# Instance norm on one core: storing finished units two at a time, in transfers of 8 MB

## The chip, the cores and the metric

The kernel runs on 1 core of one Trainium2 chip. The metric is device time in microseconds (us), the median of repeated runs. Lower is better. A transfer between device memory (HBM) and on-chip memory (SBUF) is carried by the core's 16 DMA engines, which all instructions that issue transfers share.

## The reference

Each of the 4 x 8 x 16 = 512 channels of `x` is a plane of 256 x 256 float32 values. Each plane is normalised by its own mean and variance and multiplied by one number of `gamma`:

```python
def reference(x, gamma):                  # x: (4, 8, 16, 256, 256), gamma: (8, 16)
    mu = x.mean(axis=(3, 4), keepdims=True)
    var = ((x - mu) ** 2).mean(axis=(3, 4), keepdims=True)
    x_norm = (x - mu) / np.sqrt(var + 1e-5)
    return (x_norm * gamma[None, :, :, None, None]).astype(np.float32)
```

So 134.2 MB are read and 134.2 MB are written, and every plane has to be on the chip as a whole before its first output value is known.

## The kernel before, in words

**Tiling.** The input is cut into U = 32 units of 16 planes. A plane is spread over S = 8 partitions, so a unit fills 128 partitions with F = 8192 values each: 32 KB a partition, 4 MB in all. A unit is one contiguous 4 MB piece of HBM, in the input and in the output alike.

**Buffers.** There are AHEAD = 6 slots of one unit each (`xt`). Unit u lives in slot u % 6 from its load until its store has landed, and the result is written over the input.

**Loads (L48).** The first six loads are issued at the start, those of units 1 and 3 from ScalarE's queue and the other four from SyncE's (SP). Inside the loop, SP issues the load of unit u + 6 after the store of unit u; since it fills the same slot, it waits until that store has landed. SP has no other work, and the order of its loads is the order of the units.

**Work on a unit.** VectorE sums the unit (L102) while ScalarE squares it and sums the squares (L103, its elementwise output goes to a scratch tile `junk`). A small matmul (L111) adds up the 8 partitions of each plane and hands the result to all 8. Then come four steps of one number a partition: the negated variance (L112, VectorE), its square root (L116, ScalarE), the reciprocal (L120) and the product with gamma (L122, both VectorE). Last, VectorE writes the scaled unit in place (L125).

**Stores (L129).** ScalarE's queue issues the store of unit u when L125 has finished. The next unit's squares (L103) stand behind it on ScalarE.

The instructions of each engine run in the order in which the loop writes them. Waits are on semaphores, which a transfer raises when its data have landed. Each transfer is cut by its partitions over the 16 DMA engines: 8 rows of 32 KB for each engine, and one small packet that raises the semaphore. There are two rings of such work at each DMA engine, one for SP's issues (queue q1 in the profile) and one for ScalarE's (q10).

Of the kernel before, what the change touches and what calls it, by code (L numbers as in the profile page):

```python
# [1 line left out]

# [4 lines left out]

F32 = mybir.dt.float32
U8 = mybir.dt.uint8
ALU = mybir.AluOpType  # L10
ACTF = mybir.ActivationFunctionType
AX = mybir.AxisListType


@with_exitstack
def kernel(
    ctx: ExitStack,
    tc: tile.TileContext,
    x: bass.AP,
    gamma: bass.AP,  # L20
    out: bass.AP,
):
    nc = tc.nc
    B, G, C, H, W = x.shape
    P = nc.NUM_PARTITIONS
    HW = H * W
    n_ch = B * G * C
    S = 8
    K = P // S
    F = HW // S  # L30
    U = n_ch // K
    NG = (G * C) // K
    AHEAD = 6
    assert HW % S == 0 and (G * C) % K == 0

    xv = x.rearrange("b g c h w -> (b g c h w)").rearrange("(u p f) -> u p f", p=P, f=F)
    ov = out.rearrange("b g c h w -> (b g c h w)").rearrange("(u p f) -> u p f", p=P, f=F)
    gv = gamma.rearrange("g c -> (g c)")

    data = ctx.enter_context(tc.tile_pool(name="data", bufs=1))  # L40
    singles = ctx.enter_context(tc.tile_pool(name="singles", bufs=1))
    psum = ctx.enter_context(tc.tile_pool(name="psum", bufs=4, space=bass.MemoryType.PSUM))
    ctx.enter_context(tc.manual_schedule())

    slots = [data.tile([P, F], F32, name=f"xt{i}") for i in range(AHEAD)]

    def load(u, queue):
        queue.dma_start(out=slots[u % AHEAD][:], in_=xv[u])  # L48


    g_row = singles.tile([1, G * C], F32, name="g_row")
    nc.gpsimd.dma_start(out=g_row[:], in_=gv[None, :])  # L52
    for u in range(AHEAD):
        load(u, nc.scalar if u in (1, 3) else nc.sync)


    eps_t = singles.tile([P, 1], F32, name="eps_t")
    nc.gpsimd.memset(eps_t[:], 1e-5)  # L58
    one = singles.tile([1, 1], F32, name="one")
    nc.gpsimd.memset(one[:], 1.0)  # L60
    navg = singles.tile([P, K, S], F32, name="navg")
    nc.gpsimd.memset(navg[:], -1.0 / HW)  # L62
    nc.gpsimd.affine_select(  # L63
        out=navg[:], in_=navg[:], pattern=[[-S, K], [0, S]], compare_op=ALU.is_ge,
        fill=0.0, base=0, channel_multiplier=1,
    )
    nc.gpsimd.affine_select(  # L67
        out=navg[:], in_=navg[:], pattern=[[S, K], [0, S]], compare_op=ALU.is_ge,
        fill=0.0, base=S - 1, channel_multiplier=-1,
    )  # L70
    navg_w = navg[:].rearrange("p k s -> p (k s)")
    root_eps = singles.tile([P, 1], F32, name="root_eps")
    nc.scalar.activation(out=root_eps[:], in_=eps_t[:], func=ACTF.Sqrt)  # L73
    g_rep = singles.tile([1, NG, K, S], F32, name="g_rep")
    g_ps = psum.tile([P, NG], F32, name="g_ps", bufs=1)
    g_col = singles.tile([P, NG], F32, name="g_col")

    nc.vector.tensor_copy(  # L78
        out=g_rep[:],
        in_=g_row[:].rearrange("o (n k) -> o n k", n=NG).unsqueeze(3).to_broadcast([1, NG, K, S]),  # L80
    )
    for n in range(NG):
        nc.tensor.matmul(  # L83
            out=g_ps[:, n : n + 1],
            lhsT=g_rep[:, n].rearrange("o k s -> o (k s)"),
            rhs=one[:],
            start=True, stop=True,
        )
    nc.vector.tensor_copy(out=g_col[:], in_=g_ps[:])  # L89

    junk = singles.tile([P, F], U8, name="junk")

    st = singles.tile([P, U, 2], F32, name="st")
    nvar = singles.tile([P, U], F32, name="nvar")
    std = singles.tile([P, U], F32, name="std")
    rstd = singles.tile([P, U], F32, name="rstd")
    scale = singles.tile([P, U], F32, name="scale")

    squares = []
    for u in range(U):  # L100
        t = slots[u % AHEAD]
        nc.vector.reduce_sum(out=st[:, u, 0:1], in_=t[:], axis=AX.X)  # L102
        square = nc.scalar.activation(  # L103
            out=junk[:], in_=t[:], func=ACTF.Square, accum_out=st[:, u, 1:2],
        )
        if u:

            tc.declare_no_dep(square.ins, squares[-1].ins, reason="junk, ordered by the root between")
        squares.append(square)
        ps = psum.tile([P, 2], F32, name="ps")  # L110
        nc.tensor.matmul(out=ps[:], lhsT=navg_w, rhs=st[:, u], start=True, stop=True)  # L111
        nc.vector.tensor_scalar(  # L112
            out=nvar[:, u : u + 1], in0=ps[:, 0:1], scalar1=ps[:, 0:1],
            scalar2=ps[:, 1:2], op0=ALU.mult, op1=ALU.add,
        )
        nc.scalar.activation(  # L116
            out=std[:, u : u + 1], in_=nvar[:, u : u + 1], func=ACTF.Sqrt,
            bias=eps_t[:], scale=-1.0,
        )
        nc.vector.reciprocal(out=rstd[:, u : u + 1], in_=std[:, u : u + 1])  # L120
        g = u % NG
        nc.vector.tensor_mul(  # L122
            out=scale[:, u : u + 1], in0=rstd[:, u : u + 1], in1=g_col[:, g : g + 1],
        )
        nc.vector.tensor_scalar(  # L125
            out=t[:], in0=t[:], scalar1=ps[:, 0:1], scalar2=scale[:, u : u + 1],
            op0=ALU.add, op1=ALU.mult,
        )
        nc.scalar.dma_start(out=ov[u], in_=t[:])  # L129
        if u + AHEAD < U:  # L130
            load(u + AHEAD, nc.sync)


# [1 line left out]
_INS = ['x', 'gamma']  # L135
_OUTS = [((4, 8, 16, 256, 256), 'float32')]


# [23 lines left out]
```

## Time and profile before

| what | value |
|---|---|
| median of 3 runs | 626.83 us (626.78 to 626.91) |
| span of the profiled execution, first to last instruction | 625.2 us |
| median less span: what lies around the instructions | 1.6 us |
| VectorE busy | 443.2 us (71%) |
| ScalarE busy | 238.8 us (38%) |
| TensorE busy | 21.4 us (3%) |
| moved by DMA | 268.46 MB, 429 GB/s over the span |
| mean of one L102, L103, L125 | 8.68, 7.03, 4.55 us |
| stores: count, size, median from issue to landing | 32, 4 MB, 62.5 us |
| loads: count, size, median from issue to landing | 32, 4 MB, 38.5 us (SP's 30) |

The profiled execution has no time of its own beside its span, so the 1.6 us around it are the difference to the median of the runs. In the profile, "busy" is the time in which an engine executes; the time from issue to landing of a transfer holds its wait behind earlier transfers of the same ring. The chain of waits is followed back from the last instruction, and each of its pieces says when it began, how long it lasted, and what it was.

### The profile page before, as it was taken

The page shows a single profiled execution, that of the slowest core. Times are in us where ns is not written, and L with a number is a line of the kernel's source. Part 1 is how long each engine was busy: PE and PEld are TensorE (multiplying, and loading weights), DVE is VectorE, ACT ScalarE, POOL GpSimd, SP SyncE. Part 2 cuts the span into 40 slices and gives each one's busy share as a digit, 9 for nine tenths or more (in the row PEclk, how much of TensorE's full clock was granted, in tenths as well). Part 3 has the DMA queues.
Part 4 walks back from the last instruction along what each step waited for, and adds up shares of the span by engine and source line. Part 5 has one row for each costly group of instructions (what it writes and reads, how often), then busy time and mean ns, then how long its engine had stood idle before and what let it go on. Part 6 is the DMA issues. An engine that isn't in the chain of part 4 may idle for free.

```text
span 625.2 us, 627 instructions
## 1 busy us (share of the span) xinstructions
PE 21.4 (3%) x80; PEld 19.6 (3%) x80; DVE 443.2 (71%) x162; ACT 238.8 (38%) x98; POOL 1.9 (0%) x10
## 2 busy tenths in 40 slices
PE   2000000000000000000000000000000000000000
PEld 2000000000000000000000000000000000000000
DVE  0588999999776687666786767867668676687730
ACT  0444444444443244432344423444224442244400
POOL 1000000000000000000000000000000000000000
DMA  8999999999999999999999999999999999999998
GB/s 369 436 403 436 436 436 436 436 426 432 434 434 436 424 434 436 436 434 436 436 421 434 434 434 432 432 434 436 436 434 436 436 419 434 434 436 432 432 434 369
DMA packets 9251, 268.46 MB, mean 429 GB/s; under 512 B 1057, under 2 KB 1057, under 8 KB 1057
## 3 DMA queue, kind: packets, MB, share of 16 engines
q10 hardware_dynamic: 4896, 142.61, 52.9%
q1 hardware_dynamic: 4320, 125.83, 46.8%
q14 instruction: 3, 0.02, 0.0%
q0 software_dynamic: 32, 0.00, 0.0%
HBM read 134.22 MB, written 134.22 MB: 429 GB/s over the span
## 4 chain that ended last, share of the span: by engine, by line
another core or an unknown queue 61%; DMA 17%; DVE 15%; SPq 1%; PE 1%; issue 0%; ACT 0%
DMA xt<-in_x_dram 10%; DVE st L102 10%; DMA out_dram<-xt 8%; DVE xt L125 5%; SPq L48 1%; PE ps L111 1%; ACT std L116 0%; DVE nvar L112 0%; DVE rstd L120 0%; DVE scale L122 0%
## 5 line engine op out<-in xcount | busy, mean ns | idle before, releaser
L102 DVE TENSOR_REDUCE st<-xt 128x1 f32<-128x8192 f32 x32 | 277.9, 8684 | 105.3 <-DMA xt<-in_x_dram 105.3
L103 ACT ACTIVATE junk<-xt 128x8192 uint8<-128x8192 f32 x32 | 224.9, 7029 | 275.4 <-DMA xt<-in_x_dram 232.2
L125 DVE TENSOR_SCALAR xt<-xt,ps,scale 128x8192 f32<-128x8192 f32 x32 | 145.6, 4550 | 1.2
L116 ACT ACTIVATE std<-nvar,eps_t 128x1 f32<-128x1 f32 x32 | 9.4, 294 | 79.7 <-DVE nvar L112 79.7
L111 PE MATMUL ps<-st,navg 128*128 128x2 f32 x64 | 17.9, 349 | 562.0 <-DVE st L102 562.0
L111 PEld LDWEIGHTS ps<-st,navg 128*128 128x128 f32 x64 | 16.1, 312 | 563.8 <-issue 563.8
L112 DVE TENSOR_SCALAR nvar<-ps 128x1 f32<-128x1 f32 x32 | 9.2, 287 | 23.9 <-PE ps L111 23.9
L120 DVE RECIPROCAL rstd<-std 128x1 f32<-128x1 f32 x32 | 5.3, 164 | 11.6 <-ACT std L116 11.6
L78 DVE COPY g_rep<-g_row 1x1024 f32<-1x1024 f32 x1 | 0.7, 683 | 10.6 <-DMA g_row<-in_gamma_dram 10.6
L103 ACT ACTIVATION_READ_ACCUMULATOR junk<-xt 128x1 f32 x32 | 6.0, 186 | 0.0
L122 DVE TENSOR_TENSOR scale<-rstd,g_col 128x1 f32<-128x1 f32 x32 | 5.1, 159 | 1.1
L83 PE MATMUL g_ps<-one,g_rep 1*128 1x1 f32 x16 | 3.5, 347 | 11.5 <-DVE g_rep L78 11.5
L83 PEld LDWEIGHTS g_ps<-one,g_rep 1*128 1x128 f32 x16 | 3.5, 326 | 11.4 <-issue 11.4
L89 DVE COPY g_col<-g_ps 128x8 f32<-128x8 f32 x1 | 0.2, 167 | 3.7 <-PE g_ps L83 3.7
L73 ACT ACT_TABLE_LOAD x1 | 1.3, 1283 | 1.7 <-PEq L146 1.7
L52 POOL DMA_DIRECT2D g_row<-in_gamma_dram x1 | 0.6, 607 | 0.8 <-POOLq L146 0.8
L63 POOL TENSOR_SCALAR_AFFINE_SELECT navg<-navg 128x128 f32<-128x128 f32 x1 | 0.4, 398 | 0.1
L67 POOL TENSOR_SCALAR_AFFINE_SELECT navg<-navg 128x128 f32<-128x128 f32 x1 | 0.4, 398 | 0.1
L62 POOL MEMSET navg<- 128x128 f32 x1 | 0.2, 230 | 0.0
L73 ACT ACTIVATE root_eps<-eps_t 128x1 f32<-128x1 f32 x1 | 0.2, 203 | 0.0
L58 POOL MEMSET eps_t<- 128x1 f32 x1 | 0.1, 118 | 0.0
L146 POOL MEMSET const-bfloat16-1.0<- 128x1 bf16 x1 | 0.1, 102 | 0.0
(4 smaller groups left out, 0.4 us busy)
## 6 DMA issues: line engine op xcount, KB each, us to landing
out_dram<-xt ACTq DMA_DIRECT2D x32, 4096.0 KB, 62.5
xt<-in_x_dram SPq DMA_DIRECT2D x30, 4096.0 KB, 38.5
xt<-in_x_dram ACTq DMA_DIRECT2D x2, 4096.0 KB, 31.8
g_row<-in_gamma_dram POOLq DMA_DIRECT2D x1, 0.5 KB, 9.3
```

Source lines behind the costliest of these rows:

```text
L48: queue.dma_start(out=slots[u % AHEAD][:], in_=xv[u])
L73: nc.scalar.activation(out=root_eps[:], in_=eps_t[:], func=ACTF.Sqrt)
L78: nc.vector.tensor_copy(out=g_rep[:], in_=g_row[:].rearrange("o (n k) -> o n k", n=NG).unsqueeze(3).to_broadcast([1, NG, K, S]),)
L83: nc.tensor.matmul(out=g_ps[:, n : n + 1], lhsT=g_rep[:, n].rearrange("o k s -> o (k s)"), rhs=one[:], start=True, stop=True,)
L102: nc.vector.reduce_sum(out=st[:, u, 0:1], in_=t[:], axis=AX.X)
L103: square = nc.scalar.activation(out=junk[:], in_=t[:], func=ACTF.Square, accum_out=st[:, u, 1:2],)
L111: nc.tensor.matmul(out=ps[:], lhsT=navg_w, rhs=st[:, u], start=True, stop=True)
L112: nc.vector.tensor_scalar(out=nvar[:, u : u + 1], in0=ps[:, 0:1], scalar1=ps[:, 0:1], scalar2=ps[:, 1:2], op0=ALU.mult, op1=ALU.add,)
L116: nc.scalar.activation(out=std[:, u : u + 1], in_=nvar[:, u : u + 1], func=ACTF.Sqrt, bias=eps_t[:], scale=-1.0,)
L120: nc.vector.reciprocal(out=rstd[:, u : u + 1], in_=std[:, u : u + 1])
L122: nc.vector.tensor_mul(out=scale[:, u : u + 1], in0=rstd[:, u : u + 1], in1=g_col[:, g : g + 1],)
L125: nc.vector.tensor_scalar(out=t[:], in0=t[:], scalar1=ps[:, 0:1], scalar2=scale[:, u : u + 1], op0=ALU.add, op1=ALU.mult,)
```

## The change

The six slots of one unit become three tiles of two units each; `slot(u)` names the half of such a pair that unit u lives in. The work on a unit is the same, on the same engines and in the same order. What differs is when transfers are issued and how large they are:

- An even unit is no longer stored when it is finished. After the odd unit of a pair is finished, one transfer stores both (8 MB). Its output side is written as partition, unit, value, so that each partition's row of 64 KB in SBUF goes to two rows of 32 KB that lie 4 MB apart in HBM.
- The two loads that refill the pair's tile are still 4 MB each. SP issues both after the store of the pair, and both wait for it to land.
- The last two units, 30 and 31, are stored one by one.

The first six loads, and the queues that issue them, stay as they were. There are 17 stores in place of 32, and 32 loads as before.

```diff
-    slots = [data.tile([P, F], F32, name=f"xt{i}") for i in range(AHEAD)]
+    pairs = [data.tile([P, 2, F], F32, name=f"xt{i}") for i in range(AHEAD // 2)]
+
+    def slot(u):
+        return pairs[u // 2 % (AHEAD // 2)][:, u % 2]
 
     def load(u, queue):
-        queue.dma_start(out=slots[u % AHEAD][:], in_=xv[u])
+        queue.dma_start(out=slot(u), in_=xv[u])
...
-        nc.scalar.dma_start(out=ov[u], in_=t[:])
-        if u + AHEAD < U:
-            load(u + AHEAD, nc.sync)
+        if u >= U - 2:
+            nc.scalar.dma_start(out=ov[u], in_=t)
+        elif u % 2:
+            nc.scalar.dma_start(
+                out=ov[u - 1 : u + 1].rearrange("u p f -> p u f"), in_=pairs[u // 2 % (AHEAD // 2)][:],
+            )
+            for v in (u - 1 + AHEAD, u + AHEAD):
+                if v < U:
+                    load(v, nc.sync)
```

In the changed kernel the load is line L51, the single store L133, the pair's store L135, and the in-place scaling L128.

More of the change, by code (lines that the diff above doesn't have):

```diff
@@ L100 @@
     for u in range(U):
-        t = slots[u % AHEAD]
-        nc.vector.reduce_sum(out=st[:, u, 0:1], in_=t[:], axis=AX.X)
+        t = slot(u)
+        nc.vector.reduce_sum(out=st[:, u, 0:1], in_=t, axis=AX.X)
         square = nc.scalar.activation(
-            out=junk[:], in_=t[:], func=ACTF.Square, accum_out=st[:, u, 1:2],
+            out=junk[:], in_=t, func=ACTF.Square, accum_out=st[:, u, 1:2],
         )
@@ L125 @@
         nc.vector.tensor_scalar(
-            out=t[:], in0=t[:], scalar1=ps[:, 0:1], scalar2=scale[:, u : u + 1],
+            out=t, in0=t, scalar1=ps[:, 0:1], scalar2=scale[:, u : u + 1],
             op0=ALU.add, op1=ALU.mult,
         )
-        nc.scalar.dma_start(out=ov[u], in_=t[:])
-        if u + AHEAD < U:
-            load(u + AHEAD, nc.sync)
+        if u >= U - 2:
[7 more added lines that the diff above has]
+                    load(v, nc.sync)
 _INS = ['x', 'gamma']
```

## The prediction

> **What bounds the kernel now.** I read the page's DMA rows first, because 268 MB in 625 us is a rate that may leave nothing over.
>
> ```profile
> span 625.2 us, 627 instructions
> ...
> DMA packets 9251, 268.46 MB, mean 429 GB/s; under 512 B 1057, under 2 KB 1057, under 8 KB 1057
> ...
> q10 hardware_dynamic: 4896, 142.61, 52.9%
> q1 hardware_dynamic: 4320, 125.83, 46.8%
> ...
> out_dram<-xt ACTq DMA_DIRECT2D x32, 4096.0 KB, 62.5
> xt<-in_x_dram SPq DMA_DIRECT2D x30, 4096.0 KB, 38.5
> ```
>
> The two rings' packets take 52.9 + 46.8 = 99.7% of the time of all 16 DMA engines. Whatever VectorE (71% busy) and ScalarE (38%) do is hidden; the kernel is a stream of 64 transfers of 4 MB, and only time in which the DMA engines have nothing to do can be won or lost. The last rows say that this cannot easily happen: a store lands 62.5 us after its issue, so there is always a queue. (The GB/s of the page's 40 slices jump between 436 and lower values because whole rounds of packets are counted; I read no stall from them.)
>
> Second, the chain of waits, for the pace in the middle and for the end:
>
> ```profile
> 159.90 0.33 SPq L48
> 160.23 18.97 another core or an unknown queue
> 179.20 0.02 SPq L48
> ...
> 179.25 0.33 SPq L48
> ```
>
> SP issues a load each time a store lands, and 179.25 - 159.90 = 19.35 us pass between two such landings. In each period one load and one store go through, so a transfer of 4 MB costs 9.68 us. 64 x 9.68 = 619.5 us of the span of 625.2. Of the other 5.7 us, 1.8 pass before the first packet (the packet records begin there, for loads issued at 0.81), and the rest are slow packets at the start and around 41 us, the last landing and the closing instructions. "An unknown queue" is the store ring.
>
> Third, the timeline at the start and at the end, for what the change moves:
>
> ```profile
> 37.82 0.35 ACTq L129 DMA_DIRECT2D out_dram<-xt  x1
> ...
> 52.76 0.35 ACTq L129 DMA_DIRECT2D out_dram<-xt  x1
> ...
> 67.69 0.34 ACTq L129 DMA_DIRECT2D out_dram<-xt  x1
> ...
> 78.04 4.55 DVE L125 TENSOR_SCALAR xt<-xt,ps,scale 128x8192 f32<-128x8192 f32 x1
> 81.96 0.33 SPq L48 DMA_DIRECT2D xt<-in_x_dram  x1
> ...
> 82.62 0.34 ACTq L129 DMA_DIRECT2D out_dram<-xt  x1
> ...
> 600.59 0.34 ACTq L129 DMA_DIRECT2D out_dram<-xt  x1
> ```
>
> The stores of units 0, 1, 2 and 3 are issued at 37.82, 52.76, 67.69 and 82.62: here VectorE sets the pace, one unit in 14.93 us. At 81.96 SP issues the load of unit 7, because the store of unit 1 has just landed. By then exactly eight transfers have gone through: loads 0 to 5 and stores 0 and 1. At the end the last store is issued at 600.59 and lands at 624.2, or 23.6 us later, where 9.7 would do alone: the ring still had a backlog of 14 us.
>
> **The change part by part.**
>
> *Fifteen stores fewer.* The bytes and the 32 KB packets stay; 15 x 16 semaphore packets go. In the stretch after 585 us only stores run, and there the packet records of one engine start 1.209 us apart inside a store and 1.215 us apart over the boundary of two stores. So a boundary costs 0.006 us, and 15 of them 0.09 us: -0.1. From below, even if all of the 0.3% in which the rings' packets do not fill the engines were boundaries, it would be 0.3% x 625.2 = 1.9 us for 64 transfers, 0.44 us for 15. I take -0.1, the row being the thing itself.
>
> The Trainium skill, DMA: Bandwidth & Descriptors, section on the anatomy of one DMA, fits a transfer as about 2.0 us fixed plus bytes over 436 GB/s; put on this sum it would make 15 transfers fewer worth 30 us. The trace disagrees for a ring that is never empty: 0.006 us.
>
> *The first pair's store waits for unit 1.* It is issued at about 52.8 in place of 37.82 and 52.76. The six loads keep the engines busy past that (48 rounds of 1.21 us and the start: to about 61 us), so nothing idles here. After it, loads and this store together are the same eight transfers as above. They pass through the engines without a gap, so they end when they did before: packets end on the 16 engines at 80.6 to 81.4 (mean 81.0), the landing is seen at 81.9.
>
> *The rings are then empty.* Before, three more transfers were waiting at this point: load 6 (issued when store 0 landed, at about 62.6), store 2 (67.69), and store 3 coming. After, load 6 waits for the whole pair, so SP issues it only at about 81.96 and load 7 some 0.33 us later; and units 2 and 3 leave together, not before unit 3 is scaled, at 78.04 + 4.55 = 82.6. The first load of the kernel was issued at 0.81 and its first packet began at 1.81, so an issue takes 1.0 us to reach the engines when they are idle. Load 6 starts at 81.96 + 1.0 = 83.0, store 2+3 at 82.62 + 1.0 = 83.6. The engines idle from 81.0 in the mean to 83.0: 2.0 us. This lies fully on the path, since DMA is work that nothing later can make up. If the single ring of loads (42 to 54 us) or the pair's store alone (61 to 81) should run slower than two rings do, which the trace shows only for stores, the landing would come later and the loss would grow to 83.6 - 81.0 = 2.6 and no further, until that delay itself passes 2.6. From below: 81.96 + 1.0 less the last engine's end at 81.4 is 1.6 us.
>
> *Restart.* The first packets of the kernel took 1.21 to 2.10 us, in the mean about 0.4 us more than the steady 1.213. After a pause of 2 us I expect less than from cold; 0 to 0.9 us, I take 0.2.
>
> *Later rounds.* The second rotation: pair 2 (units 4 and 5) is scaled at 82.6 + 2 x 14.93 = 112.5, while the store of pair 1 cannot land before 83.0 + 38.7 = 121.7. So the next store is in the ring 9 us before the previous one lands, and covers the 1.6 us in which SP sees the landing and gets a load to the engines. The third: pair 3 at 142.4 against a landing of pair 2 at about 161. In steady state a tile's cycle is three pairs, 3 x 38.7 = 116 us, and it needs 38.7 for its loads, 15.1 for the last unit, and 38.7 for its store: 92.5. The 23 us left are the time that stores wait in the ring, against a hand-over of 1.6. Cost nothing; if this cover were gone, each of the 13 hand-overs would cost about 2 us.
>
> *Issue on ScalarE.* A store's issue takes 0.34 us of its queue, with the next unit's squares behind it; 15 issues go, and one of two rows per partition may take up to twice as long. ScalarE is done 1.3 us before VectorE in each unit (7.03 + 0.19 us against 8.68), so either is hidden. SP's second load stands behind the first (0.33 us) and is hidden by the first one's 9.68 us.
>
> *The end.* Units 30 and 31 leave singly as before. With about 23 us of stores queued when the last one is issued, nothing idles: 0.
>
> *Rows 4 MB apart.* A store now jumps 4 MB in HBM between packets. At the start of the trace loads 0 and 1 ran side by side on the two rings, 4 MB apart in the input row by row, with packets of 1.213 us, the same as everywhere. I take 0. A page speaks against the change: the same DMA page, section on latency and other measured facts, lists a per-partition pitch of 4 MiB at half rate (103 against 214 GB/s); by it 30 units of stores would take 30 x 9.68 = 290 us more. I hold the row against it: here the pitch is between successive packets of 32 KB, not between partitions, and the two loads side by side show no slowing.
>
> **Sum.** Against the profiled execution: 625.2 - 0.1 + 2.0 + 0.2 = 627.3 us of span, and with the 1.6 us around it 628.9 us. The parts give 626.83 - 0.44 + 1.6 = 628.0 to 626.83 + 2.6 + 0.9 = 630.3. A measurement of this kernel can tell about 0.2%, or 1.25 us, from no change.
>
> **The rivals.**
>
> *Nothing to see (626.8 to 628.0).* If the issue reaches waiting engines much faster than at the cold start, in 0.3 us, the loss is 81.96 + 0.3 - 81.0 = 1.3 us less the boundaries; or if unit 3 were stored 2 us earlier, the rings would not run dry. For it: only one start stands behind the 1.0 us. Against: landing and SP's wake-up alone take 0.9 us after the mean engine's end. About 627.6; chance 0.15.
>
> *Faster: larger stores run better.* If each store taken away saved more than 2.1 / 15 = 0.14 us, the saving would outweigh the gap; at 0.25 us it would be 3.75, giving 626.83 - 3.75 + 2.2 = 625.3. For it: a store's end leaves the engines spread over nearly 1 us. Against: the other ring's packets fill that, and the boundary reads 0.006 us. Chance 0.05.
>
> *Slower by more: the store itself is slowed.* If packets that alternate between two places took 2% longer, 30 units x 9.68 x 2% = 5.8 us come on top: 634.7. Every 0.4% costs 1.2 us. For it: no store in this trace alternates. Against: the two loads side by side. Or a hand-over opens more than once, at 2 us each. Chance 0.10.
>
> **How the numbers follow.** The forecast, one gap of about 2 us, has 0.70 and 628.0 to 630.3. The range takes half of the first rival and the lower edge of the last: 627.3 to 630.8. Slower by over 0.2% (above 628.1): nearly all of the forecast and the last rival, 0.79; within: 0.16; faster: 0.05.
>
> **What would show it.** Right: the timeline shows SP issuing two loads at about 82.0 and 82.3 and no DMA packets between about 81.4 and 83; afterwards landings of pairs 38.7 us apart, and every later landing shifted by about 2.1 us; the two rings' shares sum to about 99.4%. Wrong: pair landings clearly over 38.8 us apart (the store is slowed), under 38.6 (boundaries cost more than I read), a gap at a second landing, or the first pair's store landing well after 82.

## The result, and the profile after

The changed kernel takes 641.09 us (median of 5 runs, 640.01 to 643.47) against 626.83 before: a ratio of 1.0233, 95% interval 1.0218 to 1.0249. The forecast of 628.9 had the sign and the first mechanism right, and missed some 12 us. The profiled execution has a span of 639.4 us, 14.2 more than before. How far the runs lie apart is news too: 3.5 us here, 0.14 before.

The gap came where it was expected. The timeline of the changed kernel at the end of the eighth transfer (start us, duration us, instruction):

```profile
77.89 4.55 DVE L128 TENSOR_SCALAR xt<-xt,ps,scale 128x8192 f32<-128x8192 f32 x1
81.87 0.80 SPq L51 DMA_DIRECT2D xt<-in_x_dram  x2
...
82.48 0.40 ACTq L135 DMA_DIRECT2D out_dram<-xt  x1
```

Both loads are issued at 81.87 and the store of units 2 and 3 at 82.48, when nothing is left in either ring. The windows around it, first of the kernel before, then of the changed one (the last two columns are the mean busy share of the 16 DMA engines and GB/s):

```profile
81.00:83.00 2.00, 0.00 (x0) 0.00 (x0) 2.00 (x2) 0.00 (x0) 0.00 (x0) 1.00 0.84 360
83.00:88.00 5.00, 0.00 (x0) 0.00 (x0) 5.00 (x1) 5.00 (x1) 0.00 (x0) 1.00 0.98 419
```

```profile
81.00:83.00 2.00, 0.00 (x0) 0.00 (x0) 2.00 (x2) 0.08 (x1) 0.00 (x0) 1.00 0.57 147
83.00:88.00 5.00, 0.00 (x0) 0.00 (x0) 5.00 (x1) 5.00 (x1) 0.00 (x0) 1.00 0.88 301
```

Two microseconds are a coarse window for packets of 1.2; the packet records say 2.01 us without a packet in the mean of the 16 engines. The window after it is the first surprise: the engines are 88% busy and still move only 301 GB/s. The restart is slow.

The larger surprise stands in a window over the middle of the run. Before, then after:

```profile
118.00:620.00 502.00, 14.53 (x52) 13.05 (x52) 354.19 (x130) 187.72 (x78) 0.00 (x0) 1.00 1.00 433
```

```profile
118.00:620.00 502.00, 14.51 (x52) 13.03 (x52) 349.96 (x130) 187.62 (x78) 0.00 (x0) 1.00 1.00 425
```

The DMA share is 1.00 in both. No engine idles, and yet 8 GB/s are gone: 8 / 433 x 502 = 9.3 us. The same bytes, in the same 8192 packets of 32 KB, keep the engines busy for longer. The DMA rows of the page answer to those of before:

```profile
span 639.4 us, 587 instructions
...
DMA packets 9010, 268.46 MB, mean 420 GB/s; under 512 B 816, under 2 KB 816, under 8 KB 816
...
q10 hardware_dynamic: 4656, 142.61, 52.1%
q1 hardware_dynamic: 4320, 125.83, 47.0%
...
xt<-in_x_dram SPq DMA_DIRECT2D x30, 4096.0 KB, 41.8
out_dram<-xt ACTq DMA_DIRECT2D x15, 8192.0 KB, 44.9
```

The 241 small packets fewer are there (9251 to 9010), so the change did what it says. The two rings still fill 52.1 + 47.0 = 99.1% of the engines' time, now of a longer span. The loads' ring has the same 4320 packets as before and takes 47.0% of 639.4 us where it took 46.8% of 625.2: 300.5 us for each engine in place of 292.6.

From the records of single packets the 14.2 us come apart as follows. A packet of 32 KB takes 1.213 us in the steady state of both kernels; "slow" is what a packet takes above that, summed and divided by 16 engines.

| part | before | after | difference |
|---|---|---|---|
| no packet on the engines around 81 us | 0 | 2.0 | 2.0 |
| slow packets up to 80 us (the start, the first store) | 1.4 | 1.6 | 0.2 |
| slow packets at the restart, 80 to 90 us | 0.0 | 1.4 | 1.3 |
| slow packets from 120 us on | 0.1 | 8.9 | 8.8 |
| engines done before the last one, at the end | 0.5 | 2.1 | 1.6 |

That makes 13.9 of the 14.2; the rest is not assigned. The slow packets from 120 us on come in bursts near the landing of a pair's store, of up to 38 packets over the 16 engines; about 7 of the 8.9 us lie in the ten microseconds before it lands, so most bursts begin before SP issues the next loads. About three in four of the slow packets are loads that are still under way. A packet in a burst takes 1.3 to 2.9 us.

### The profile page after: what moved, and what is told of

It reads as the page before. It is cut to its first block, busy times and chain, and to the rows that moved or that the text cites. A ratio compares the mean times of both kernels' runs of the same rounds, so it can differ in the third digit from the quotient of the medians.

```text
span 639.4 us, 587 instructions
## 1 busy us (share of the span) xinstructions
PE 21.4 (3%) x80; PEld 19.5 (3%) x80; DVE 443.3 (69%) x162; ACT 238.5 (37%) x98; POOL 1.9 (0%) x10
## 2 busy tenths in 40 slices
DMA packets 9010, 268.46 MB, mean 420 GB/s; under 512 B 816, under 2 KB 816, under 8 KB 816
## 3 DMA queue, kind: packets, MB, share of 16 engines
q10 hardware_dynamic: 4656, 142.61, 52.1%
q1 hardware_dynamic: 4320, 125.83, 47.0%
## 4 chain that ended last, share of the span: by engine, by line
DMA 59%; DVE 27%; another core or an unknown queue 9%; PE 1%; issue 1%; ACT 1%; SPq 0%
DMA xt<-in_x_dram 31%; DMA out_dram<-xt 27%; DVE st L105 18%; DVE xt L128 9%; PE ps L114 1%; ACT std L119 1%; DVE nvar L115 1%; DVE rstd L123 0%; DVE scale L125 0%; SPq L51 0%
## 5 line engine op out<-in xcount | busy, mean ns | idle before, releaser
L128 DVE TENSOR_SCALAR xt<-xt,ps,scale 128x8192 f32<-128x8192 f32 x32 | 145.6, 4551 | 1.2
L123 DVE RECIPROCAL rstd<-std 128x1 f32<-128x1 f32 x32 | 5.2, 164 | 11.6 <-ACT std L119 11.6
```

The costliest lines, as they stand in the source:

```text
L128: nc.vector.tensor_scalar(out=t, in0=t, scalar1=ps[:, 0:1], scalar2=scale[:, u : u + 1], op0=ALU.add, op1=ALU.mult,)
```

## The experiments

Each is a small edit of the changed kernel, unless it says otherwise. Times are medians against runs of the kernel before on the same chip. "Middle" is the GB/s of the window from 118 to 620 us, read as above (433 before, 425 after).

**The same schedule with stores of 4 MB.** In place of the pair's store:

```diff
+            for v in (u, u - 1):
+                nc.scalar.dma_start(out=ov[v], in_=slot(v))
```

The odd unit goes first, so that the even unit's refill, which SP issues first, still waits for the whole pair.

> The pair still leaves at once and its loads still wait for the whole pair, but as two stores of 4 MB (odd unit first), each contiguous in HBM, in place of one of 8 MB. Theory A (the schedule slows it: the load ring runs dry at each hand-over, and packets are slow when it starts again): as the changed kernel, 639 to 643 us, with 8 to 12 us of slow packets per engine. Theory B (the large store is slow in itself, because its packets alternate between rows 4 MB apart or because there are 16 rows per engine): 628 to 630 us, the gap at 81 us alone being left.

Measured: 631.16 us, ratio 1.0063 (1.0048 to 1.0079), middle 433. The rows and the waits are the same; one transfer has become two, which also puts the rows in another order (see below). 10 of the 14 us are gone. Between 80 and 90 us it still has 1.8 us without packets and 1.5 us of slow ones; after 90 us the slow ones come to 0.1 us. SP's issues at the hand-overs show it; two of the changed kernel, then the same two of this run:

```profile
158.84 0.82 SPq L51 DMA_DIRECT2D xt<-in_x_dram  x2
...
551.98 0.86 SPq L51 DMA_DIRECT2D xt<-in_x_dram  x2
```

```profile
160.08 0.86 SPq L51 DMA_DIRECT2D xt<-in_x_dram  x2
...
547.32 0.80 SPq L51 DMA_DIRECT2D xt<-in_x_dram  x2
```

Ten hand-overs lie between: 38.72 us for each with two stores, exactly four transfers of 9.68, and 39.31 with one. The schedule theory falls: the waits are the same here, and no bursts come of them. Its premise fails too, already in the changed kernel. When SP issues the two loads at 158.84, the second load of the pair before has not landed yet; VectorE can begin on that unit only at 170.14:

```profile
158.84 0.82 SPq L51 DMA_DIRECT2D xt<-in_x_dram  x2
...
170.14 8.69 DVE L105 TENSOR_REDUCE st<-xt 128x1 f32<-128x8192 f32 x1 [4.81 <-DMA xt<-in_x_dram]
```

So the load ring is not dry at this hand-over. By the landing records it had run dry at the one before (last load landed at 122.6, next issued at 123.91), and at none after it.

With the even unit's store first, its refill leaves earlier:

> As the run of two contiguous stores a pair, but the even unit's store goes first and its load waits for it alone, so that one load is issued about 10 to 19 us before the other and the load ring need not run dry. Theory A (load ring runs dry): most of the slow packets go, 628 to 631 us. Theory B (large store): 628 to 630 us as well; it differs from theory A only through the run in which both loads wait.

Measured: 629.32 us, but from 627.32 to 633.72; ratio 1.0043 (1.0022 to 1.0064), middle 433. No bursts, as both theories said. The records of this execution (span 631.2) lose 5.9 us at the end, where the engines finish up to 7 us apart. In this execution the loss is a spread of the engines and not of the packets; the other runs left no records.

**Is it the jump of 4 MB?** Three runs. The stores were written elsewhere in the output, once with the two rows of a partition 33 KB apart, once with the second unit 36 KB further on:

```diff
-                out=ov[u - 1 : u + 1].rearrange("u p f -> p u f"), ...
+                out=pair_out(u // 2), ...
...
+        return bass.AP(tensor=flat.tensor, offset=flat.offset + n * 2195456, ap=[[17152, P], [8448, 2], [1, F]])
```

> The changed kernel with its 8 MB stores put elsewhere in the output: the two 32 KB rows of a partition go 33 KB apart, the partitions 67 KB apart (the output is misplaced, units 30 and 31 go over the first two pairs; all bytes and waits are as in the changed kernel). No packet jumps by 4 MB, the size of a store stays 8 MB. If the alternation over 4 MB makes the packets slow: 630 to 632 us, as with two contiguous stores. If it is the size of a store (16 rows an engine): 639 to 643 us.

Measured: 639.52 us, ratio 1.0205 (1.019 to 1.022), middle 426.

> The changed kernel with the second unit of each pair written 36 KB further on, so that the packets of a store alternate over 4 MB + 36 KB (the output is misplaced, units 30 and 31 go over the start). If it is the power of two in the pitch: 630 to 632 us. If any alternation between two far places, or the size of a store, makes the packets slow: 639 to 643 us.

Here the last line read `n * 2106368, ap=[[8192, P], [1057792, 2], [1, F]]`. Measured: 639.65 us, ratio 1.0212 (1.0188 to 1.0237), middle 424. And the reverse, a jump of 4 MB in stores of 4 MB:

```diff
+            for h in (0, F // 2):
+                nc.scalar.dma_start(
+                    out=ov[u - 1 : u + 1, :, h : h + F // 2].rearrange("u p f -> p u f"),
+                    in_=pairs[u // 2 % (AHEAD // 2)][:, :, h : h + F // 2],
+                )
```

> The pair leaves at once as two stores of 4 MB with all 128 partitions: the first half of each row of both units, then the second half, in packets of 16 KB that alternate over 4 MB. If the alternation makes packets slow: 639 us or more. If it is the size of one store: 630 to 633 us.

Measured: 631.84 us, ratio 1.0079 (1.0062 to 1.0095), middle 432. Without the jump of 4 MB the kernel is slow, and with it, in stores of 4 MB (and packets of 16 KB), it is not. Neither the far jump nor the power of two is the cause, and the row that the prediction set against the page on pitches was the right one to follow.

**A miss: halves by partitions.** Each pair in two stores of 64 partitions and both units:

> The pair leaves as two stores of 4 MB, but each holds 64 partitions of both units, so that packets alternate between rows 4 MB apart as in the changed kernel. Theory A (schedule): 639 to 643 us. Theory B, if it is the alternation: 639 to 643 too; if it is the size of one transfer: 628 to 630 us. Together with the run of two contiguous stores this parts schedule, alternation and size.

Measured: 715.85 us, ratio 1.1437 (1.1367 to 1.1506). Neither theory had this. A window in which only stores run, up to about 97 us:

```profile
68.00:100.00 32.00, 1.15 (x4) 1.01 (x4) 27.77 (x11) 14.99 (x7) 0.00 (x0) 1.00 1.00 217
```

The engines are fully busy at 217 GB/s: a store packet of 32 KB takes 2.39 us here, twice the 1.21 of a store over 128 partitions. The Trainium skill, DMA: Bandwidth & Descriptors, rules for kernel authors, advises against two transfers to disjoint partition halves, because they serialize; this run shows worse than that, since a half alone gets only half the rate. As a test of alternation it says nothing.

**The gap by itself, twice.** First in the kernel before, with the stores of units 0 and 1 issued together, and those of 2 and 3:

> The kernel before, with one edit: the stores of units 0 and 1 are both issued after unit 1, those of units 2 and 3 both after unit 3, all later stores singly. This makes the gap of about 2 us at 81 us without large stores or later pairs. If the gap costs what was forecast and nothing follows from it: 626.8 + 2.0 = 628.8 us (628.2 to 629.6). If the gap itself upsets the order of the two rings for the rest of the run (slow packets at later hand-overs): 633 us or more.

Measured: 628.26 us (627.32 to 631.72), ratio 1.0026 (1.0012 to 1.004). The number fits and the reason does not: SP issued the load of unit 6 at 73 us in this run, so there was no gap at 81, only 0.5 us more of slow packets. I had not seen that store 0, alone in its transfer, lands early and lets load 6 go. The run shows nothing about the gap. The second way was to take the gap out of the changed kernel:

```diff
+        if u < 2:
+            nc.scalar.dma_start(out=ov[u], in_=t)
+            load(u + AHEAD, nc.sync)
+        elif u >= U - 2:
```

> The changed kernel, but units 0 and 1 leave singly, each with its own refill, so that load 6 is in its ring when the eighth transfer ends. The gap at 81 us and the restart after it (2.0 + 1.4 us in the changed kernel's packet records) should go: 636 to 639 us if the slow packets of the later hand-overs stay. If they came from the gap, 628 us.

Measured: 635.89 us (634.03 to 638.91), ratio 1.0149 (1.0117 to 1.0181), middle 424. The gap is gone from the records, the bursts stay, so they do not come from it. And with the later pairs in two stores of 4 MB as well:

> Units 0 and 1 leave singly with their own refills, and every later pair leaves at once as two stores of 4 MB. This undoes the gap and the large store, and keeps the pairs' schedule: if these two are all, 627 to 628 us. If pairing costs something beside them (load ring dry at each hand-over): 630 us or more.

Measured: 627.18 us, ratio 1.0015 (0.9991 to 1.0039), middle 433; nine of the ten runs took 626.93 to 627.74 us, one 634.65, of which there are no records. The traced run, one of the nine:

```profile
81.00:83.00 2.00, 0.00 (x0) 0.00 (x0) 2.00 (x2) 0.00 (x0) 0.00 (x0) 1.00 0.76 328
...
118.00:620.00 502.00, 14.53 (x52) 13.02 (x52) 354.10 (x130) 189.09 (x78) 0.00 (x0) 1.00 1.00 433
```

This kernel keeps pairs, waits for whole pairs and refills them at once, and it is within the error of the kernel before. So the pairs' schedule costs nothing that shows (the interval ends at 0.4%), and the four kernels make a table: neither gap nor large store 1.0015, the gap alone 1.0063, the large store alone 1.0149, both 1.0233.

**Smaller packets, and large loads.** One store of 8 MB in packets of 16 KB, and two stores of 4 MB with one load of 8 MB a pair:

> One store of 8 MB a pair as in the changed kernel, but in packets of 16 KB (33 a partition's four pieces apart by 16.5 KB, the output is misplaced; units 30 and 31 go over the first pairs). Beside the run with two stores of half rows (631.8 us, also 16 KB packets) only the number of transfers differs. If it is the single large transfer: 636 to 643 us. If a large transfer is slow only with packets of 32 KB: 630 to 633 us.

Measured: 635.62 us (633.16 to 635.96), ratio 1.0137 (1.0121 to 1.0154); the profiled execution was the quickest of them, and its middle is 432, with about 1.2 us of slow packets after 90 us in place of 8.9. The median lies just under the range set for a guilty large transfer, the records look like an innocent one. This run is inconclusive.

> The pair leaves at once as two stores of 4 MB, and its two refills are one load of 8 MB. If any transfer of 8 MB makes packets slow: 638 to 645 us. If only large stores do: 631 us, or up to 634 since the first unit of a pair now waits for the whole load.

Measured: 636.17 us, ratio 1.0145 (1.013 to 1.016), middle 430, and no bursts after 145 us. Its loss lies at the two ends: 2.3 us around 81 us, and 5.3 us without packets after 615 us, because units 30 and 31 land together and are stored only at 606.14 and 621.08, when the ring has run out. So "any transfer of 8 MB" is not the rule; the bursts are shown for the store, in packets of 32 KB.

One rival to the size of that store is not tested. As its access pattern is written, the two 32 KB rows of a partition follow each other in the store of 8 MB; in two contiguous stores of 4 MB a whole unit goes first and then the other. The two runs with packets of 16 KB have the pieces of a partition in succession in both, and neither trace was slow, but no run with packets of 32 KB and 128 partitions parts the size of a store from the order of its rows. What is shown is that a pair stored as one transfer costs the time, and stored as two does not.

**Without any compute.** What stayed open was whether such a store slows packets in itself or only at a hand-over, and whether the engines' work on the buffers has a part in it. Four plain copies. In the first two, stores and loads wait for nothing of each other; in the last two, a pair is stored when it has been loaded and refilled when it has been stored:

```diff
+        for h in (0, 1):
+            nc.sync.dma_start(out=t[:, h], in_=xv[2 * n + h])
+        nc.scalar.dma_start(out=ov[2 * n : 2 * n + 2].rearrange("u p f -> p u f"), in_=t[:])
```

> No compute: 32 units are loaded into four rotating buffers that nobody reads, and two further units, loaded once, are stored 16 times as pairs of 8 MB; stores and loads do not wait for each other, and both rings always hold work. 66 transfers of 4 MB at 9.68 us make a floor of 639 us, 642 with start and end. If a store of 8 MB slows packets beside loads in itself: 650 us or more, and clearly above the same with 4 MB stores. If only the hand-over does: within 2 us of it.

> As the free copy with 8 MB stores, but each pair leaves as two stores of 4 MB: 641 to 645 us by either theory; it is the control.

> The changed kernel's tiles and transfers without compute: the pair is stored (8 MB) when both its loads have landed, and refilled when its store has landed; the input is copied. If hand-overs of a large store are enough to make packets slow: 6 us or more of slow packets in its records, 632 us or more in all. If it takes the engines' work on the buffers, or the finely timed issue that it sets: no slow packets after the start.

> The copy by pairs without compute, but each pair leaves as two stores of 4 MB, odd unit first, so that both refills still wait for the whole pair. If the large store is what makes packets slow at the hand-over: 433 GB/s in the middle of the run in place of 424, and 630 to 639 us in all in place of 646. If any hand-over of a whole pair does it when no compute spaces the issues: 424 GB/s and 645 us again.

Measured: free copies 654.37 us (650.45 to 662.91) with 8 MB and 645.73 (645.68 to 646.54) with 4 MB; copies by pairs 646.44 (645.25 to 648.23) and 626.46 (626.30 to 626.91). The middle of the two copies by pairs, 8 MB first (without compute, the columns are time, GpSimd, clock, share and GB/s):

```profile
40.00:600.00 560.00, 0.00 (x0) 1.00 1.00 424
600.00:643.50 43.50, 0.00 (x0) 1.00 0.80 345
```

```profile
40.00:600.00 560.00, 0.00 (x0) 1.00 1.00 433
600.00:624.40 24.40, 0.00 (x0) 1.00 0.92 398
```

The whole effect is there without one compute instruction: 9 GB/s over 560 us, 11.6 us, and a burst at nearly every hand-over (13.5 us of slow packets in all, against 1.4). The other 7 of the 19 us between the two spans lie at the end: with 8 MB the engines drift until they land one transfer up to 24 us apart, with 4 MB never over 0.6. One store of 8 MB or two of 4 MB, with the order of rows that goes with it, is the only difference. Where stores wait for nothing, the 8 MB run meets by its median the range set for a store that is slow in itself (650 us or more), but its records have just two such bursts, at 100 and 440 us (middle 431 against 433), and loses 4.2 us at the end (1.0 with 4 MB), where its engines finish apart; its runs lie 12 us apart, and the records are of one of them. So in these traces a hand-over of a large store brings the bursts about regularly, and a large store beside independent loads now and then.

What inside the DMA engines makes them is open. Landings show the 16 engines drifting: in the changed kernel the first and the last engine end a transfer mostly 0.5 us apart up to 124 us and up to 7 us apart after 330 us, with two stores of 4 MB never over 2.8. But the run with the even unit's store first drifted to 10 us without a burst, so drift alone is not the cause.

## Why the prediction was wrong

- **The gap: right.** Place (81 us), cause (both rings empty), SP's issue (82.0 forecast, 81.87 measured), the store's (82.62, 82.48) and the size (2.0, 2.01).
- **Restart: mis-sized.** The term was 0.2 us with a bound of 0.9. It measured 1.4, two slow packets on each engine of about 0.65 each, and 1.5 with two stores of 4 MB. The first is the first load packet. The second is a load packet again, just before the first store packet comes in. The trace before held both prices: 0.47 us a packet at the cold start, and 0.9 us of slow packets at 39 to 43 us, where the first store came in beside loads. The prediction scaled the one down for a short pause, and named the other ("around 41 us") without putting it into the term.
- **"Later rounds: cost nothing": right as a wait, and it hid the error.** No engine idles at a later hand-over, as worked out, and the pairs' schedule by itself costs nothing (1.0015). But the prediction started from "only time in which the DMA engines have nothing to do can be won or lost", priced the hand-over by idle time alone, and carried 9.68 us a transfer over unchanged. The engines lost 8.9 us from 120 us on while they were busy.
- **The step that failed is the price of the pair's store as one transfer.** The sum holds it as a saving (fifteen boundaries, -0.1 us) and as a jump of 4 MB (0, which holds), never as something that makes packets slow. It cost 8.8 us in slow packets, and about 0.9 us more at the end than two stores do (2.1 against 1.2). The third rival, "the store itself is slowed", had the direction and a chance of 0.10, but through packets that alternate between two places; with the two places 33 KB apart the time stayed at 639.52 us. And it is mostly the loads beside the store that are slow.
- **The page on bandwidth.** The fit in the Trainium skill, DMA: Bandwidth & Descriptors, would have made fewer transfers worth an estimated 30 us. The page gives it for transfers that GpSimd issues; here SP and ScalarE issue them. The row said 0.1; the runs say that from 4 to 8 MB it goes the other way.
- **The test I had set** caught it: pair landings "clearly over 38.8 us apart", here 39.31.

## What to carry to other kernels

When the DMA engines are busy for 99% of the span, read GB/s next to the busy share in a window of the steady state: a packet that takes longer counts as busy, and idle time says nothing of it. Merging transfers that are already 4 MB had nothing left to save here, and it joined what had been two early landings into one late one; if a buffer needs pairs, let each half leave by itself, and in the first rotation, while the rings are short, also refill by itself (627.18 us for a kernel of this kind, against 641.09). Size a transfer only as far as the profile shows a price at its boundaries.

## What was not expected of the hardware

- One store of 8 MB in 32 KB packets, handed over to loads, in place of two of 4 MB: 424 to 426 GB/s in place of 433, with bursts in which packets take 1.3 to 2.9 us for 1.213. Loads of 8 MB showed none after 145 us.
- Rings that start again after both were empty: about 1.4 us of slow packets for each engine, on top of the pause.
- A store from 64 of the 128 partitions: 217 GB/s with all 16 engines busy.
